# The opening of a two-layer hybrid decoder trunk: a written-out instruction order, three blocks' modulation on TensorE, and six tiles in place of four

## Chip, core and metric

One core of a Trainium2 chip runs the whole kernel in one launch. The metric is device time in microseconds, as the median of several runs. Each kernel also has one profiled execution, whose trace the views are taken from.

## The reference

A trunk of two layers works on 512 tokens of 1024 features. Each layer is a SwiGLU feed-forward step, a token mixer (windowed attention, RWKV-7 and a short convolution side by side) and a second feed-forward step. Ahead of each of the three stands an RMS norm with scale and shift that come from a conditioning vector c, and behind it a gate from c:

```python
c_act = jax.nn.silu(c)
mod = (c_act @ w_ada[l] + b_ada[l]).reshape(B, N_MOD, D_MODEL)
sh1, sc1, gt1, sh2, sc2, gt2, sh3, sc3, gt3 = [mod[:, i, None, :] for i in range(N_MOD)]
hn = rms_norm(h, g_ffn1[l]) * (1.0 + sc1) + sh1
h = h + 0.5 * (1.0 + gt1) * swiglu(hn, w_ffn1_in[l], w_ffn1_out[l])
```

All is float32. The change touches only the start of layer 0: the first norm, its scale and shift, and the first columns of `swiglu`'s first product.

## The kernel before

**Layout.** Features lie on the 128 partitions and tokens along the free axis, so `h` is eight blocks `h[0]` to `h[7]` of 128x512. A normalized block k is kept as two parts, `hnH` (rounded) and `hnL` (the rest), and so is each weight slice (`wH`, `wL`). A product of weights and blocks is then three matmuls: high by high, high by low, low by high (`mm3`, L118 to L120). A **tile** n is 128 output columns of the feed-forward's input weights: 8 blocks x 3 products = 24 matmuls of 512 columns into one PSUM bank. Even tiles are gates, odd ones are ups; a pair makes one silu product.

**The opening** (`begin`, from L1309) has to bring the first tiles to TensorE. In turn it

- replicates c over the partitions (eight matmuls, L1369) and applies silu into `crep`,
- squares the blocks on ScalarE (L243), adds the squares on VectorE (L239), and sums over the partitions with four matmuls (`ps_ss`, L1388); then square root on ScalarE (L1391), reciprocal on VectorE (L1392), and 1/rms is spread over the partitions by four matmuls (`ps_rstd`, L1395),
- forms scale and shift of the blocks: `scales` and three of four `shifts` are dot products of a streamed weight tile `wada` with `crep` on VectorE (L188); each second shift is eight one-column matmuls (`ps_ada`, L1345),
- applies them: `z` = h x 1/rms on VectorE (L1350), scale and shift on ScalarE (L1352), and the split into `hnH` (ScalarE, L130) and `hnL` (VectorE, L132); the weight splits go through the same two lines,
- runs tiles 0 to 3, four blocks' pairs after each other (m = 0 to 3), 96 matmuls.

Matmuls on a tile of ones (`warm`, L1361) fill gaps on TensorE. SP's queue issues the loads: x, then `wada` and the four `wfirst` weight slices in turns.

**Behind it** comes the first feed-forward (`ffn`). Its `projector` takes the four accumulators and goes on with tile 4; each tile's weights are loaded on SP's queue (L292), split on ScalarE and VectorE (L130, L132) into one of four buffer pairs, and multiplied. With each pair of tiles VectorE does a silu product (L513) and its split (L515). At pairs 2 and 3 (j of 2 and 3, of 8) `ada_steps` computes the gate's eight modulation columns: four dot products on VectorE each time, with `wada` tiles that GpSimd's queue loads (L199) into three slots, and with `crep` read back from DRAM (L194), where the opening stored it (L1371). The scheduler behind the tile framework sets the order on each engine from the order of the code and the dependencies; each engine runs its own list in order.

Of the kernel before, what the change touches and what calls it, by code (L numbers as in the profile page):

```python
# [8 lines left out]
F32 = mybir.dt.float32  # L9
# [22 lines left out]
PAD = 24  # L32
GROUPS = ((0, 12), (12, 22))
# [26 lines left out]
def trunk_kernel(ctx, tc, ins, out, layers=L, phases=("ffn1", "mix", "ffn2")):  # L60
# [280 lines left out]
    def ffn(l, w_in, w_pair, w_out, hn, im, ss, need, then, first, ready, coming):  # L341
# [6 lines left out]
        with tc.tile_pool(name="act", bufs=1) as ap_:  # L348
# [153 lines left out]
            for g, (j0, j1) in enumerate(GROUPS):  # L502
                for p in range(j0 // 2, j1 // 2):
                    if p < n_first:
                        X = new_x(p)
                        for j in (2 * p, 2 * p + 1):
# [10 lines left out]
                            if n_first == 4:  # L517
                                ada_steps(ap_, crep, (0, 0, 4, 4, 0, 0, 0, 0)[j], behind)
# [789 lines left out]
    def begin(pool):  # L1308
# [3 lines left out]
        col = {n: pool.tile([P, KD], F32, name=n, tag=n) for n in ("sc", "sh", "gb", "gm0", "sh0")}  # L1312
        stt(col["gb"], bsc, 1.0, g1, ALU.add, ALU.mult)
        wa, wf, ws = {}, [], []

        def fetch(m):
            for n in (0, 2):
                w = pool.tile([P, 2, D], F32, name="wada", tag="wada", bufs=8)
                nc.sync.dma_start(w, ins["wa0"][m, :, n : n + 2])
                wa[m, n], wa[m, n + 1] = w[:, 0], w[:, 1]  # L1320
# [7 lines left out]
        def split_w(n):  # L1328
            pair = tuple(wp.tile([P, KD, P], F32R, name=x, tag=x, bufs=4) for x in ("wH", "wL"))
            split(*pair, wf[n])  # L1330
            ws.append(pair)

        def scales(m):
            for n in range(2):
                k = slice(2 * m + n, 2 * m + n + 1)
                ada_dot(col["sc"][:, k], wa[m, n], crep)
                stt(col["gm0"][:, k], col["sc"][:, k], g1[:, k], col["gb"][:, k], ALU.mult, ALU.add)

        def shifts(m):
            k0, k1 = (slice(2 * m + n, 2 * m + n + 1) for n in range(2))  # L1340
            ada_dot(col["sh"][:, k0], wa[m, 2], crep)
            tt(col["sh0"][:, k0], col["sh"][:, k0], bsh[:, k0], ALU.add)
            pt = psum([P, 1], "ps_ada")
            for k in range(KD):
                mm(pt, wa[m, 3][:, k * P : (k + 1) * P], cact[:, k : k + 1], start=k == 0, stop=k == KD - 1)  # L1345
            tt(col["sh0"][:, k1], pt, bsh[:, k1], ALU.add)

        def normed(k):
            z = E("z")
            tt(z, h[k], rstd, ALU.mult)  # L1350
            x = E("hn_t")
            act(x, z, AF.Identity, bias=col["sh0"][:, k : k + 1], scale=col["gm0"][:, k : k + 1])  # L1352
            split(*hn[k], x)

        pw = psum([P, T], "ps_warm", "r1")
        wide = ones_r.unsqueeze(1).to_broadcast([P, 4, P])

        def warm(n):

            for _ in range(n):  # L1360
                mm(pw.rearrange("p (a b) -> p a b", b=P), ones_r, wide, start=True, stop=True)  # L1361

        warm(3)

        crep = pool.tile([P, D], F32, name="crep", tag="crep")
        for hf in range(2):
            pt = psum([P, 4, P], "ps_crep")
            for k in range(4):
                mm(pt[:, k], cT[:, 4 * hf + k : 4 * hf + k + 1].to_broadcast([P, P]), cst("ident"), start=True, stop=True)  # L1369
            act(crep[:, hf * 512 : hf * 512 + 512], pt.rearrange("p k n -> p (k n)"), AF.Silu)  # L1370
# [9 lines left out]
        nc.sync.dma_start(con[:, P:], ins["con"][:, P:])  # L1380
        warm(20)
        ss = new_ss()
        for i in range(KD):
            add_ss(ss, i)

        pt = psum([P, NB], "ps_ss")
        for b in range(NB):
            mm(pt[:, b : b + 1], ss[:, b * P : (b + 1) * P], ones[:, :1], start=True, stop=True)  # L1388
        warm(3)
        r = pool.tile([P, NB], F32, name="rstd_t", tag="rstd_t")  # L1390
        act(r, pt, AF.Sqrt, bias=vals["eps"], scale=1.0 / D)  # L1391
        nc.vector.reciprocal(r, r)  # L1392
        rstd = psum([P, T], "ps_rstd", "r0")
        for b in range(NB):
            mm(rstd[:, b * P : (b + 1) * P], r[:, b : b + 1].to_broadcast([P, P]), cst("ident"), start=True, stop=True)  # L1395
        warm(2)
        scales(0)
        shifts(0)
        warm(8)
        normed(0)  # L1400
        split_w(0)
        split_w(1)
        normed(1)
        pts = [psum([P, T], "ps_mm", tag) for tag in ("mm", "mm", "r1", "r0")]
        for m in range(4):
            groups = [(n, 2 * m + k) for k in range(2) for n in range(4)]
            if m == 0:
                groups = [(n, k) for n0 in (0, 2) for k in range(2) for n in (n0, n0 + 1)]
            elif m == 3:
                groups = [(n, 6 + k) for n in range(4) for k in range(2)]  # L1410
            for g, (n, k) in enumerate(groups):
                mm3(pts[n], ws[n], k, hn[k], ALL, k == 0, k == KD - 1)
                if m < 3 and g == 1:
                    scales(m + 1)
                    shifts(m + 1)
# [120 lines left out]
```

## Time and profile before

| | |
|---|---|
| median of 3 runs | 1811.94 us (1808.89 to 1813.52) |
| profiled execution | 1810.68 us, span 1808.9 us |
| mean granted TensorE clock | 0.996 |
| TensorE, VectorE, ScalarE, GpSimd busy | 98%, 75%, 46%, 8% of the span |
| chain that ended last | TensorE 85%, VectorE 8%, ScalarE 3%, DMA 2% |

The granted clock is the share of full speed that TensorE was allowed in a stretch. The chain that ended last follows the last instruction back, at each step to what released it. In rows of the timeline stand start, duration, engine, line, operation, output and inputs, shapes and count, and in brackets how long the engine had been idle and what ended that.

### The profile page before, as it was taken

How to read it: one execution, taken by the hardware profiler on the slowest of the kernel's cores; microseconds unless marked ns; L12 is line 12 of the kernel's file. 1: busy time of each engine (PE TensorE's matmuls, PEld its weight loads, DVE VectorE, ACT ScalarE, POOL GpSimd, SP SyncE). 2: the span in 40 equal slices, each digit the busy share in tenths (PEclk: the TensorE clock that was granted, in tenths of full speed). 3: DMA queues.
4: the chain of work that ended last, by engine and by line, in shares of the span. 5: the costliest groups of instructions: out<-in, count | busy, mean ns of one | idle time of the engine just before them, and what ended most of it. 6: DMA issues, size and time to landing. Idle time of an engine off the chain costs nothing.

```text
span 1808.9 us, 33704 instructions
## 1 busy us (share of the span) xinstructions
PE 1779.8 (98%) x13856; PEld 1624.5 (90%) x13856; DVE 1353.8 (75%) x2188; ACT 839.8 (46%) x1292; POOL 141.9 (8%) x225
## 2 busy tenths in 40 slices
PE   8999999999999999999999999999999999999999
PEld 6899899987768999899899989999877799999998
DVE  7687677877768877777877786877696698864862
ACT  4443255374443554255355524544654445533541
POOL 0001110101000001100100010110000000010000
PEclk9999999999999999999999999999999999999999
DMA  8667876713123576967737687773321427684742
GB/s 330 227 166 222 258 193 199 239 65 94 62 84 119 152 192 197 297 180 200 247 110 202 171 293 199 192 229 120 123 65 40 137 83 200 183 247 129 197 140 71
DMA packets 91980, 309.93 MB, mean 171 GB/s; under 512 B 10480, under 2 KB 11248, under 8 KB 90800
## 3 DMA queue, kind: packets, MB, share of 16 engines
q1 hardware_dynamic: 62496, 201.58, 32.6%
q0 software_dynamic: 29328, 106.18, 23.4%
q8 instruction: 109, 1.79, 0.4%
q14 instruction: 47, 0.39, 0.1%
HBM read 303.79 MB, written 3.93 MB: 170 GB/s over the span
## 4 chain that ended last, share of the span: by engine, by line
PE 85%; DVE 8%; ACT 3%; DMA 2%; issue 1%; POOL 0%; ACTq 0%; DVEq 0%; SPq 0%; POOLq 0%
PE ps_mm L118 14%; PE ps_mm L119 14%; PE ps_mm L120 14%; PE ps_d L422 7%; PE ps_d L424 7%; PE ps_d L423 7%; PE ps_f L424 3%; PE ps_f L423 3%; PE ps_f L422 3%; PE ps_g L424 2%; PE ps_g L423 2%; PE ps_g L422 2%; DVE wL L132 2%; DVE wada L188 1%; ACT wH L130 1%
## 5 line engine op out<-in xcount | busy, mean ns | idle before, releaser
L130 ACT CAST wH<-wraw 128x1024 fp32r<-128x1024 f32 (+2 forms) x292 | 266.0, 917 | 466.7 <-PE ps_mm L119 219.0
L132 DVE TENSOR_TENSOR wL<-wraw,wH 128x1024 fp32r<-128x1024 f32 (+2 forms) x292 | 308.3, 1060 | 118.9 <-ACT wH L130 117.5
L118 PE MATMUL ps_mm<-actH,wH 128*128 128x512 f32 (+1 forms) x784 | 281.0, 358 | 0.0
L120 PE MATMUL ps_mm<-actH,wL 128*128 128x512 f32 (+1 forms) x784 | 280.6, 358 | 0.0
L119 PE MATMUL ps_mm<-actL,wH 128*128 128x512 f32 (+1 forms) x784 | 280.5, 358 | 0.0
L118 PE MATMUL ps_mm<-hnH,wH 128*128 128x512 f32 (+1 forms) x760 | 266.1, 357 | 7.1 <-ACT hnH L130 2.9
L119 PE MATMUL ps_mm<-hnL,wH 128*128 128x512 f32 (+1 forms) x760 | 265.9, 352 | 0.3
L120 PE MATMUL ps_mm<-hnH,wL 128*128 128x512 f32 (+1 forms) x760 | 264.0, 350 | 0.6 <-DVE wL L132 0.6
L422 PE MATMUL ps_d<-comH,wH 128*128 128x256 f32 x816 | 225.2, 276 | 0.0
L423 PE MATMUL ps_d<-comL,wH 128*128 128x256 f32 x816 | 224.4, 275 | 0.0
L424 PE MATMUL ps_d<-comH,wL 128*128 128x256 f32 x816 | 224.4, 275 | 0.0
L188 DVE SCALAR_TENSOR_TENSOR wada<-wada,crep 128x1024 f32<-128x1024 f32 x140 | 167.6, 1219 | 30.0 <-DMA wada<-in_wadaT 29.9
L132 DVE TENSOR_TENSOR wL<-sum,wH 128x1024 fp32r<-128x1024 f32 x102 | 125.0, 1225 | 85.4 <-ACT wH L130 85.4
L118 PEld LDWEIGHTS ps_mm<-hnH,wH 128*128 128x128 f32 x760 | 142.9, 191 | 30.0 <-issue 7.6
L120 PEld LDWEIGHTS ps_mm<-actH,wL 128*128 128x128 f32 x784 | 148.7, 190 | 16.9 <-DVE wL L132 0.3
L118 PEld LDWEIGHTS ps_mm<-actH,wH 128*128 128x128 f32 x784 | 148.7, 190 | 16.6
L119 PEld LDWEIGHTS ps_mm<-actL,wH 128*128 128x128 f32 x784 | 148.7, 190 | 16.6
L120 PEld LDWEIGHTS ps_mm<-hnH,wL 128*128 128x128 f32 x760 | 145.4, 191 | 15.6 <-DVE wL L132 1.1
L119 PEld LDWEIGHTS ps_mm<-hnL,wH 128*128 128x128 f32 x760 | 145.3, 191 | 15.5 <-DVE hnL L281 1.0
L422 PEld LDWEIGHTS ps_d<-comH,wH 128*128 128x128 f32 x816 | 156.6, 192 | 1.6 <-ACT s L448 1.6
L424 PEld LDWEIGHTS ps_d<-comH,wL 128*128 128x128 f32 x816 | 156.7, 192 | 0.0
L423 PEld LDWEIGHTS ps_d<-comL,wH 128*128 128x128 f32 x816 | 156.6, 192 | 0.0
(366 smaller groups left out, 3742.9 us busy)
## 6 DMA issues: line engine op xcount, KB each, us to landing
wada<-in_wadaT POOLq DMA_DIRECT2D x128, 512.0 KB, 4.7
wraw<-in_wmi SPq DMA_DIRECT2D x40, 512.0 KB, 3.5
wraw<-in_w2p SPq DMA_DIRECT2D x36, 512.0 KB, 4.4
wraw<-in_w1p SPq DMA_DIRECT2D x32, 512.0 KB, 4.5
wraw<-in_w1o SPq DMA_DIRECT2D x32, 384.0 KB, 4.6
wraw<-in_w2o SPq DMA_DIRECT2D x32, 384.0 KB, 4.3
wraw<-in_w1i SPq DMA_DIRECT2D x20, 512.0 KB, 4.7
wraw<-in_w1o SPq DMA_DIRECT2D x32, 320.0 KB, 3.8
```

Source lines behind the costliest of these rows:

```text
L118: mm(acc, wH, xH, start=start, stop=False)
L119: mm(acc, wH, xL, start=False, stop=False)
L120: latest["large"] = mm(acc, wL, xH, start=False, stop=stop)
L130: nc.scalar.copy(hi, src)
L132: return nc.vector.tensor_sub(lo, src, hi.bitcast(F32))
L188: stt(w, w, 1.0, crep, ALU.mult, ALU.mult, accum_out=out_)
L422: mm(acc, wH, xH, start=start and i + k == 0, stop=False, skip_group_check=True)
L423: mm(acc, wH, xL, start=False, stop=False, skip_group_check=True)
L424: mm(acc, wL, xH, start=False, stop=k == 3, skip_group_check=True)
```

## The change

`begin` is rewritten. Its loops are replaced by a table `PLAN`, a list of 213 short tokens; a function `step` emits one instruction (or a small group) per token, and `pin` ties each instruction on TensorE, VectorE and ScalarE to the one before it on its engine, so that each engine's list is the order of the table. The tokens: `z`, `x`, `H`, `L` with a block number are the multiplication by 1/rms, scale and shift, and the two halves of the split; `wH`, `wL` with a tile number the weight split; `P13c` is tile 1, block 3, third product; `W4` four warm-up matmuls; `d`, `e` the dot products for scale and shift of a block.

- Blocks 0, 1 and 2 get scale and shift from TensorE: `ada` streams a block's 256 modulation columns through eight float32 matmuls of 32 output rows each, which go in turns to four groups of 32 partitions of one bank; `part` copies the bank to SBUF, `col` sums it over the partitions, `gm` adds gain and bias. The stationary operand is `cz`, silu(c) in every 32nd column and zeros between. Blocks 3 to 7 have two dot products each on VectorE.
- The sum of squares stays on TensorE: every block's squares go through four one-column matmuls of their own (32 instead of 4). ScalarE and VectorE share the squares.
- Six tiles (0 to 5) instead of four are computed in the opening, so `projector` goes on with tile 6. The accumulators take all six banks of three PSUM tags.
- x is loaded in four pairs of blocks, `wada` and the six `wfirst` slices one after the other; six of these loads wait for a buffer of an earlier one.
- `crep` is stored to DRAM behind the opening's last VectorE instruction instead of at its start.
- The eight gate columns in `ffn` move from j of 2 and 3 to j of 0 and 1.

```diff
+PLAN = """
+z0 ada0 z1 z7 part0 wH0 W1 col0 z6 gm0 z2 W4 ada1 z4 x0 z3 H0 wL0 part1 P00a wH1 col1 L0 P00c P10a gm1 P00b P10b wL1 x1 ada2 H1 z5 P10c part2 P01a L1
...
-    for i in range(KD):
-        t = hp_.tile([P, T], F32, name=f"h{i}")
-        nc.sync.dma_start(t, ins["xT"][i])
-        h.append(t)
+    for i in range(0, KD, 2):
+        t = hp_.tile([P, 2, T], F32, name=f"h{i}")
+        nc.sync.dma_start(t, ins["xT"][i // 2])
+        h += [t[:, 0], t[:, 1]]
...
-                                ada_steps(ap_, crep, (0, 0, 4, 4, 0, 0, 0, 0)[j], behind)
+                                ada_steps(ap_, crep, (4, 4, 0, 0, 0, 0, 0, 0)[j], behind)
...
+        def pin(e, m):
+            if e in behind:
+                tc.add_manual_dep(m.ins, behind[e].ins.name, ORDER, reason="the opening keeps its order")
+            behind[e] = m
+            return m
...
+        cz = pool.tile([P, KD, CH // 2], F32, name="cz", tag="cz")
+        nc.gpsimd.memset(cz, 0.0)
+        nc.gpsimd.tensor_copy(cz[:, :, 0], cact)
...
-        nc.gpsimd.dma_start(silu_c, crep)
-        fetch(0)
-        fetch_w()
-        fetch_w()
-        fetch(1)
-        fetch_w()
-        fetch_w()
-        fetch(2)
-        fetch(3)
-        warm(20)
-        ss = new_ss()
-        for i in range(KD):
-            add_ss(ss, i)
-        for b in range(NB):
-            mm(pt[:, b : b + 1], ss[:, b * P : (b + 1) * P], ones[:, :1], start=True, stop=True)
...
+        for _ in range(4):
+            fetch()
+            fetch_w()
+        def summed(i):
+            for b in range(NB):
+                m = mm(pt[:, b : b + 1], sqs[i][:, b * P : (b + 1) * P], ones[:, :1], start=i + b == 0, stop=i == KD - 1, skip_group_check=True)
+                pin("PE", m)
+        summed(0)
+        summed(1)
+        for i in range(2, KD):
+            sqs.append(E("sq"))
+            if i in (5, 7):
+                pin("ACT", act(sqs[i], h[i], AF.Square))
+            else:
+                pin("DVE", tt(sqs[i], h[i], h[i], ALU.mult))
+            if i % 2 == 0:
+                warm(4)
+            summed(i)
+        warm(3)
...
-        pts = [psum([P, T], "ps_mm", tag) for tag in ("mm", "mm", "r1", "r0")]
-        for m in range(4):
...
+        more = {"ada0": (fetch,), "ada1": (fetch, fetch_w), "ada2": (fetch,), "wL1": (fetch_w,), "e3": (fetch,)}
...
+            elif kind == "ada":
+                sums[k] = psum([P, 2 * P], "ps_ada")
+                for i in range(KD):
+                    j = slice(i % 4 * 32, i % 4 * 32 + 32)
+                    pin("PE", mm(sums[k][j], cz[:, i], wa[k][:, i * 2 * P : (i + 1) * 2 * P], start=i < 4, stop=i >= 4))
+            elif kind == "part":
+                part[k] = pool.tile([P, 2 * P], F32, name="part", tag="part", bufs=2)
+                pin("ACT", nc.scalar.copy(part[k], sums[k]))
+            elif kind == "col":
+                sums[k] = psum([P, 2], "ps_col")
+                for i in range(2):
+                    pin("PE", mm(sums[k][:, i : i + 1], part[k][:, i * P : (i + 1) * P], ones[:, :1], start=True, stop=True))
+            elif kind == "gm":
+                finish(c, sums[k][:, :1], sums[k][:, 1:])
...
+        for token in PLAN:
+            step(token)
+        kept = nc.gpsimd.dma_start(silu_c, crep)
+        tc.add_manual_dep(kept.ins, behind["DVE"].ins.name, SYNC, reason="after the opening's loads")
+        return hn, [pts[n] for n in range(6)]
```

What this makes of the lists of instructions is seen best at two places. TensorE from the replication of c (`ps_crep`) to the first main matmuls (`ps_mm`), before:

```order
L1369 MATMUL ps_crep<-con,cT 128x128 x8
L1361 MATMUL ps_warm<-ones_r 128x512 x25
L1388 MATMUL ps_ss<-ones_r,ss 128x1 x4
L1361 MATMUL ps_warm<-ones_r 128x512 x8
L1395 MATMUL ps_rstd<-con,rstd_t 128x128 x4
L1345 MATMUL ps_ada<-cact,wada 128x1 x8
L118 MATMUL ps_mm<-hnH,wH 128x512 x2
L119 MATMUL ps_mm<-hnL,wH 128x512
```

The same stretch of TensorE with the change (row counts are matmuls; a float32 matmul shows as two in the trace):

```order
L1360 MATMUL ps_crep<-con,cT 128x128 x8
L1374 MATMUL ps_ss<-ones_r,sq 128x1 x8
L1350 MATMUL ps_warm<-ones_r 128x512 x4
L1374 MATMUL ps_ss<-ones_r,sq 128x1 x8
L1350 MATMUL ps_warm<-ones_r 128x512 x4
L1374 MATMUL ps_ss<-ones_r,sq 128x1 x8
L1350 MATMUL ps_warm<-ones_r 128x512 x4
L1374 MATMUL ps_ss<-ones_r,sq 128x1 x8
L1350 MATMUL ps_warm<-ones_r 128x512 x3
L1394 MATMUL ps_rstd<-con,rstd_t 128x128 x4
L1442 MATMUL ps_ada<-wada,cz 32x256 x8
L1350 MATMUL ps_warm<-ones_r 128x512
```

The sums of squares moved in between the warm-ups, eight groups of four, and the modulation of block 0 is one stream of 256 columns behind the spread of 1/rms.

VectorE behind the opening's last `hnL`, before: `wL` are the weight splits of tiles 4 and up, `wada` the gate's dot products.

```order
L132 TENSOR_TENSOR wL<-wraw,wH 128x1024
L513 SCALAR_TENSOR_TENSOR silu<-silu,ps_mm 128x512 x2
L132 TENSOR_TENSOR wL<-wraw,wH 128x1024
L515 TENSOR_TENSOR actL<-silu,actH 128x512 x2
L132 TENSOR_TENSOR wL<-wraw,wH 128x1024 x3
L513 SCALAR_TENSOR_TENSOR silu<-silu,ps_mm 128x512
L132 TENSOR_TENSOR wL<-wraw,wH 128x1024
L515 TENSOR_TENSOR actL<-silu,actH 128x512
L188 SCALAR_TENSOR_TENSOR wada,mod_2_594<-wada,crep 128x1024 x3
L132 TENSOR_TENSOR wL<-wraw,wH 128x1024
```

With the change VectorE's list at the same place starts with tile 6's split:

```order
L141 TENSOR_TENSOR wL<-wraw,wH 128x1024
L522 SCALAR_TENSOR_TENSOR silu<-silu,ps_mm 128x512 x3
L524 TENSOR_TENSOR actL<-silu,actH 128x512
L141 TENSOR_TENSOR wL<-wraw,wH 128x1024
L524 TENSOR_TENSOR actL<-silu,actH 128x512
L197 SCALAR_TENSOR_TENSOR wada,mod_2_585<-wada,crep 128x1024
L524 TENSOR_TENSOR actL<-silu,actH 128x512
L197 SCALAR_TENSOR_TENSOR wada,mod_2_585<-wada,crep 128x1024 x2
L141 TENSOR_TENSOR wL<-wraw,wH 128x1024
L197 SCALAR_TENSOR_TENSOR wada,mod_2_585<-wada,crep 128x1024
L141 TENSOR_TENSOR wL<-wraw,wH 128x1024
```

Before, the splits of tiles 4 to 9 stood ahead of the first gate dot; now those of tiles 6 and 7 do, and three dots stand ahead of tile 8's split, a fourth ahead of tile 9's.

More of the change, by code (lines that the diff above doesn't have):

```diff
@@ L1326, in fetch_w @@
             wf.append(w)
[L1328 to L1355, printed above, removed]
+        pw = psum([P, T], "ps_warm", "mm")
         wide = ones_r.unsqueeze(1).to_broadcast([P, 4, P])
```

120 lines of the change are left out of this document (77 added, 43 removed).

## The prediction

> **What bounds the kernel now.** I read the page's head first, for the size of the thing.
>
> ```profile
> span 1808.9 us, 33704 instructions
> PE 1779.8 (98%) x13856; PEld 1624.5 (90%) x13856; DVE 1353.8 (75%) x2188; ACT 839.8 (46%) x1292; POOL 141.9 (8%) x225
> ```
>
> TensorE (PE) is busy 98% of the span. The profiled execution took 1810.68 us, its span and 1.8 us around it; the three timed runs have their median at 1811.94, 1.3 above. All that the change rewrites lies in the first 4% of the span, so I cut the opening into slices, and then asked whom PE waits for in the first 160 us (beside 2.4 us for the first instruction of all).
>
> ```profile
> 0.00:15.00 15.00, 12.62 (x55) 10.99 (x56) 5.38 (x15) 10.08 (x16) 0.90 (x5) 1.00 0.85 303
> 15.00:20.00 5.00, 3.94 (x30) 3.60 (x29) 4.99 (x12) 0.52 (x1) 0.00 (x0) 1.00 1.01 419
> 20.00:25.00 5.00, 3.03 (x6) 2.05 (x7) 3.74 (x5) 4.04 (x6) 0.00 (x0) 0.69 1.01 422
> 25.00:30.00 5.00, 3.83 (x25) 3.23 (x23) 5.00 (x13) 1.70 (x2) 0.00 (x0) 0.97 1.03 422
> 30.00:35.00 5.00, 3.85 (x11) 3.17 (x12) 4.92 (x6) 2.96 (x5) 0.00 (x0) 0.71 1.01 418
> 35.00:40.00 5.00, 5.00 (x31) 4.50 (x31) 2.85 (x9) 0.00 (x0) 0.00 (x0) 0.95 0.96 383
> ```
>
> ```profile
> PE ps_mm L118 <- ACT hnH L130: 2.9, 1, 2.9
> PE ps_mm L118 <- ACT wH L130: 2.5, 2, 2.3
> ```
>
> The columns are PE, weight load, VectorE (DVE), ScalarE (ACT), GpSimd, then the granted PE clock, the DMA share and GB/s. From 15 to 35 us PE is idle 5.4 us, 5.4 us of it in waits for normalized blocks and split weights, and in two slices its clock stands at 0.69 and 0.71, which loses another 5 x 0.31 + 5 x 0.29 = 3.0 us. DVE is full there. The end of this stretch is the place to compare: when are the first six tiles (0 to 5, 24 matmuls each) done?
>
> ```profile
> 54.98 0.38 PE L118 MATMUL ps_mm<-hnH,wH 128*128 128x512 f32 x1
> ...
> 61.89 0.38 PE L120 MATMUL ps_mm<-hnH,wL 128*128 128x512 f32 x1
> ```
>
> The first row is tile 4's first matmul, the second stands 32 matmuls later: 6.91 / 32 = 0.216 us each. Before, tiles 4 and 5 end 48 matmuls after 54.98, at **65.35 us**. From there the order of the matmuls is the same in both kernels, and those waits were all up to 160 us. So the gain is 65.35 minus the new end of six tiles, called T6, less what later tiles give back.
>
> **The change, step by step.** First the way to 1/rms.
>
> ```profile
> 3.83 3.62 PE L1369 MATMUL ps_crep<-con,cT 128*128 128x128 f32 x16
> 7.10 6.45 PE L1361 MATMUL ps_warm<-ones_r 128*128 128x512 f32 x25
> 13.38 1.03 PE L1388 MATMUL ps_ss<-ones_r,ss 128*128 128x1 f32 x8
> 14.28 2.09 PE L1361 MATMUL ps_warm<-ones_r 128*128 128x512 f32 x8
> 16.20 1.05 PE L1395 MATMUL ps_rstd<-con,rstd_t 128*128 128x128 f32 x8
> ```
>
> ```profile
> 14.45 0.26 ACT L1391 ACTIVATE rstd_t<-ps_ss,v_eps 128x4 f32<-128x4 f32 x1 [1.95 <-PE ps_ss L1388]
> 14.75 0.18 DVE L1392 RECIPROCAL rstd_t<-rstd_t 128x4 f32<-128x4 f32 x1 [1.44 <-ACT rstd_t L1391]
> ```
>
> ```profile
> 17.37 0.68 DVE L1350 TENSOR_TENSOR z<-h,ps_rstd 128x512 f32<-128x512 f32 x1
> 17.97 1.22 DVE L188 SCALAR_TENSOR_TENSOR wada<-wada,crep 128x1024 f32<-128x1024 f32 x1
> ```
>
> The additions at L239 leave DVE, and PE sums each block's squares instead: eight groups like the one at 13.38, one after the other (the next row begins 0.90 after it, so 0.90 each), with twelve warm-up matmuls between them. They cannot start before the replication of c ends, at 7.45. 7.45 + 8 x 0.90 + 12 x 0.216 = 17.25; square root and reciprocal take 0.44, with their handovers 0.6, and the replication of 1/rms 1.05: z begins near **19.1 instead of 17.37**. This step loses 1.7 us. The table load for the square root goes earlier, beside the wait for blocks, and costs nothing. The paired loads of x move the same bytes, and GpSimd, 8% busy, has filled cz long before 18 us: nothing either; a late cz would delay the first stream one for one.
>
> Then block 0's modulation. DVE did it before, with dot products like the one at 17.97 (a z takes 0.60 from its start to the next instruction's, a dot 1.14 by the same measure). What follows it on ACT and DVE stays, in the durations of these rows:
>
> ```profile
> 19.48 0.81 ACT L1352 ACTIVATE hn_t<-z,sh,gm 128x512 f32<-128x512 f32 x1 [4.77 <-DVE sh L1342]
> 20.20 1.03 ACT L130 CAST wH<-wfirst 128x1024 fp32r<-128x1024 f32 x1
> 21.14 0.61 ACT L130 CAST hnH<-hn_t 128x512 fp32r<-128x512 f32 x1
> 21.26 1.23 DVE L132 TENSOR_TENSOR wL<-wfirst,wH 128x1024 fp32r<-128x1024 f32 x1 [1.28 <-ACT wH L130]
> ```
>
> For the new part, the nearest rows are a later product in two column groups, and a copy of 256 columns out of PSUM:
>
> ```profile
> 1419.38 1.08 PE L650 MATMUL ps_av<-pmc,V 128*64 128x512 f32 x4
> 1420.29 1.03 PE L650 MATMUL ps_av<-pmp,V 128*64 128x512 f32 x4
> ```
>
> ```profile
> L1173 ACT COPY Sc<-ps_sc x24: 372/376/379, 452.3 to 1399.2; 128x256 f32<-128x256 f32 x24
> ```
>
> The new streams (eight float32 matmuls of 32 output rows by 256 columns, two passes each) stand nowhere in this trace. A float32 pass takes twice a column's normal time (0.216 per 512), so 256 columns take 0.216 a pass. Bounds: one after the other, 16 x 0.216 = 3.5 us; four column groups fully side by side, 0.9. The nearest row is ps_av: four passes of 512 columns in two groups of 64, 0.91 us from first to next, where in sequence they would take 1.7. So groups do run beside each other, and I take **1.0** with the switch. By the Trainium skill's "TensorEngine Tiling (Array Packing)", Key Properties, changing the tiling mode drains TensorE, which speaks against three short streams among full-width matmuls; if each of six switches cost the 0.16 by which a matmul's 0.38 exceeds its pitch, that is 1.0, and 0.7 more than the 0.1 a stream that I count; no row here shows such an order.
>
> Onward: PE streams block 0 from 18.9 to 19.9; ACT copies the sums (0.38, to 20.35); two column sums on PE to 20.85. DVE does four z meanwhile (4 x 0.60, to 21.5), then scale and shift (0.3): 21.8. ACT: 0.81 and 0.61, so the first main matmul starts at **23.3**. DVE follows with three z, wL, hnL, block 1's scale and shift, wL, z and hnL: 3 x 0.60 + 1.14 + 0.60 + 0.30 + 1.14 + 0.60 + 0.60 = 6.2, to 28.0, and in that time PE does two more streams, the column sums and eight main matmuls, with gaps. From then on I find every operand ready before its turn: 136 matmuls and three warm-ups, 139 x 0.216 = 30.0, give **T6 = 58.1**. The thinnest margin is tile 3's low weights, 0.2 us ahead; for what slips I add 0.4: **58.5**.
>
> DMA hides: eight streams of 1.05 MB, six tiles of 0.52 MB and 2.3 MB of inputs are 13.8 MB. Adding up the slices above, 13.0 MB had moved by 35 us and 14.9 by 40, so the last stream lands near 38; its dot product's turn is near 43. On SP's queue these loads wait for ada0, wL0, ada1, wL1, ada2 and block 3's second dot, done by 33 us. Cover gone, each microsecond of lateness is a microsecond of T6.
>
> So the opening gains 65.35 - 58.5 = 6.85 us. Now what comes after. Tile 6's weights wait for tile 0's buffer, as tile 4's did; no change. But the eight gate columns' dots move two tile pairs up, and their loads, POOL's and the reload of c on SP, now wait for T6, because they fall on memory that the opening's last matmul reads.
>
> ```profile
> 48.56 0.33 SPq L194 DMA_DIRECT2D crep<-silu_c  x1
> ```
>
> ```profile
> 48.85 1.58 POOL L199 DMA_DIRECT2D wada<-in_wadaT  x3 [39.76 <-ACT hn_t L1352]
> 71.87 0.53 POOL L199 DMA_DIRECT2D wada<-in_wadaT  x1 [21.44 <-DVE wada L188]
> 73.02 0.53 POOL L199 DMA_DIRECT2D wada<-in_wadaT  x1 [0.62 <-DVE wada L188]
> 74.17 0.53 POOL L199 DMA_DIRECT2D wada<-in_wadaT  x1 [0.62 <-DVE wada L188]
> ```
>
> ```profile
> 76.33 1.23 DVE L188 SCALAR_TENSOR_TENSOR wada<-wada,crep 128x1024 f32<-128x1024 f32 x1 [1.32 <-DMA wada<-in_wadaT]
> ...
> 81.75 1.23 DVE L188 SCALAR_TENSOR_TENSOR wada<-wada,crep 128x1024 f32<-128x1024 f32 x1 [0.51 <-DMA wada<-in_wadaT]
> ```
>
> ```profile
> wada<-in_wadaT POOLq DMA_DIRECT2D x128, 512.0 KB, 4.7
> ```
>
> Before, the first of these loads went out at 48.9, and the reload of c at 48.6, some 20 us ahead of need. Now DVE meets the dots with the loads just issued; queued behind them on DVE are the weight splits of tiles 8 to 11, for which PE waits. From a load's issue to its dot, L, it took 4.5 us for the fourth (71.87 to 76.33) and 7.6 for the sixth (74.17 to 81.75), where DVE stood waiting for them; the median of all 128 loads is 4.7. Three slots serve eight dots, so tile 10's split comes three rounds after T6: 3L + 6.0 (three dots of 1.14, two reissues estimated at 0.4, one subtraction of 0.60, the split of 1.14, and 0.1 to start), and PE wants it at T6 + 4 x 5.18 + 0.43 = T6 + 21.2. With L = 5.06 that is even; each 1 us more costs 3. I take L = 5.4, between the median and the mean of the three (5.6): **1.0 us** given back (0 to 7.6). Tile 8's split is then 0.1 from its limit, and the Strassen-like pairs after tile 15 have DVE some 5 us less ahead than before, which I count within that range.
>
> Sum: 1810.68 - 6.85 + 1.0 = 1804.8, forecast **1805** (1806.1 set against the median instead).
>
> **The rivals.**
>
> Given back: L = 7.5 as in the slowest row holds tile 10 for 7 us; time about 1811. For it: one of two rows, and in the new order the reload of c and two weight loads share the DMA engines. Against: the median of 128. 15%.
>
> The streams don't overlap: 3 x 2.5 = 7.5 us more, T6 = 66, time 1812, so the change doesn't do what it says. Against it stands ps_av. 7%.
>
> The clock: between 8 and 17 us PE now runs 1.8 us of one-column sums to every 0.86 of warm-ups. Before, the slices that fell to 0.69 and 0.71 followed about 2 us of small matmuls and idling, and each cost 1.5 us. Three such falls in the new opening cost 4.5: 1809.3. By the Trainium skill's "TensorE: Matmul & The Clock Gate", Part 1, a free-running window of about 3.4 us decides and an idle one halves the clock; whether one-column matmuls count as idle it doesn't say, and no row here isolates them. 8%.
>
> Slower: the same place, one mechanism: if the gate loads take L = 9.2 us or more, tile 10 waits 12.4, which eats the 6.85 and 5.5 on top: 1816 and up. It decides from L = 9.2; the longest seen is 7.6. 8%.
>
> **How the numbers follow.** Forecast 62%, its own range 1801 to 1806: T6 may be 2 us earlier if nothing slips and nothing is given back, or a little later. The three middle cases, 30%, end from 1809 to 1812, and the last has 8%. A 0.3% step, 5.4 us, is about what a measurement of this kernel can tell from no change: faster 0.62, within it 0.30, slower 0.08. The range of 8 in 10 takes in the middle cases and, below, a T6 of 56 with a run at the low end of the three (3 us under the median): 1798.5 to 1813.
>
> **What would show it.** z starts at 19 (wrong if at 17 or 21); a stream takes about 1.0 on PE; first main matmul at 23 to 24; six tiles done at 58 to 59; granted clock 1.0 from 20 to 35; PE's only later waits for wL at tiles 8 and 10, a microsecond in all. A stream of 3 us, cold slices before 30, or waits of several microseconds between 69 and 85 would prove the forecast wrong, each with its rival; so would late streams on DVE near 40 (a DMA bound).

## The result: slower by 0.44%, and the profile after

The changed kernel took 1819.59 us (median of 11 runs, 1815.97 to 1822.75) against 1811.68 (11 runs, 1808.89 to 1815.70): a ratio of **1.0044, 95% interval 1.0033 to 1.0055**. Its profiled run took 1815.97 us, the fastest of the eleven. The same slices of the opening, with the columns as before:

```profile
0.00:15.00 15.00, 12.62 (x63) 11.79 (x63) 2.88 (x9) 8.03 (x12) 0.71 (x6) 0.87 0.85 324
15.00:20.00 5.00, 5.00 (x21) 4.61 (x21) 0.00 (x0) 0.00 (x0) 0.00 (x0) 0.50 1.00 408
20.00:25.00 5.00, 5.00 (x21) 4.71 (x22) 0.23 (x2) 0.26 (x1) 0.00 (x0) 0.50 0.83 338
25.00:30.00 5.00, 5.00 (x31) 2.83 (x29) 3.33 (x8) 1.85 (x3) 0.00 (x0) 0.69 0.14 34
30.00:35.00 5.00, 4.75 (x44) 2.52 (x44) 5.00 (x10) 3.88 (x7) 0.00 (x0) 1.00 0.92 370
35.00:40.00 5.00, 5.00 (x27) 4.35 (x26) 4.55 (x8) 3.50 (x5) 0.00 (x0) 1.00 0.99 388
```

TensorE is busy all through, and yet the stretch is lost: its clock stands at 0.50 from about 11 us to 28 (17.1 us by the record), and VectorE and ScalarE have next to nothing to do from 14 us until 23. The timeline of TensorE and the milestones (z, the first stream, the first main matmul, tile 6's first matmul, and VectorE's reciprocal in the norm behind the feed-forward, which stood at 360.26 before):

```profile
7.24 2.05 PE L1374 MATMUL ps_ss<-ones_r,sq 128*128 128x1 f32 x16
9.14 1.17 PE L1350 MATMUL ps_warm<-ones_r 128*128 128x512 f32 x4
...
14.43 3.41 PE L1374 MATMUL ps_ss<-ones_r,sq 128*128 128x1 f32 x16
17.70 2.05 PE L1350 MATMUL ps_warm<-ones_r 128*128 128x512 f32 x4
19.55 3.41 PE L1374 MATMUL ps_ss<-ones_r,sq 128*128 128x1 f32 x16
...
26.08 1.94 PE L1442 MATMUL ps_ada<-wada,cz 128*32 128x256 f32 x16
...
30.08 1.07 PE L1442 MATMUL ps_ada<-wada,cz 128*32 128x256 f32 x16
31.08 0.48 PE L1419 MATMUL ps_mm<-hnH,wH 128*128 128x512 f32 x1
```

```profile
26.19 2.48 DVE L1425 TENSOR_TENSOR z<-h,ps_rstd 128x512 f32<-128x512 f32 x4 [2.67 <-PE ps_rstd L1394]
```

```profile
65.89 0.46 PE L127 MATMUL ps_mm<-hnH,wH 128*128 128x512 f32 x1
```

```profile
365.56 0.17 DVE L274 RECIPROCAL rstd<-rstd 128x2 f32<-128x2 f32 x1 [1.78 <-ACT rstd L273]
```

Two blocks' eight sums (sixteen rows) take 1.9 us at 7.24 and 3.3 at 14.43, counted from a row's start to the next. Six tiles are done at 65.89, 0.5 later than before instead of 6.85 earlier, and by the first norm the kernel is 5.3 behind, which is the whole difference of the two profiled runs (1815.97 - 1810.68 = 5.29). So 4.8 us go between 66 and 366. They show as waits of TensorE, slice by slice and row by row:

```profile
60.00:100.00 40.00, 36.94 (x170) 31.55 (x169) 25.81 (x38) 14.82 (x19) 4.25 (x8) 1.00 0.62 217
100.00:140.00 40.00, 38.99 (x254) 35.95 (x253) 35.59 (x43) 21.54 (x26) 3.96 (x5) 1.00 0.70 186
```

```profile
78.72 0.48 PE L129 MATMUL ps_mm<-hnH,wL 128*128 128x512 f32 x1 [1.79 <-DVE wL L141]
90.61 0.48 PE L129 MATMUL ps_mm<-hnH,wL 128*128 128x512 f32 x1 [1.27 <-DVE wL L141]
```

The same slices before were full:

```profile
60.00:100.00 40.00, 40.00 (x187) 35.04 (x186) 32.66 (x48) 14.19 (x18) 4.37 (x7) 1.00 0.76 228
100.00:140.00 40.00, 39.99 (x284) 37.66 (x283) 30.92 (x34) 21.99 (x28) 2.23 (x3) 1.00 0.53 153
```

The waits are 3.1 + 1.0 = 4.1 us; the other 0.7 is spread too thin to be located. The 3.1 stand at tiles 8 and 10 (78.72 and 90.61), behind splits that VectorE reaches late; the 1.0 stands in the pair stage, near 128 us. That VectorE is late, and not the weights, shows at tile 8: ScalarE has the high half of its weights ready at 70.2, but VectorE works off three dots first, and the third of them has to wait for its load before tile 8's split comes.

```profile
69.20 1.04 ACT L139 CAST wH<-wraw 128x1024 fp32r<-128x1024 f32 x1
```

```profile
76.30 1.23 DVE L197 SCALAR_TENSOR_TENSOR wada<-wada,crep 128x1024 f32<-128x1024 f32 x1 [0.65 <-DMA wada<-in_wadaT]
...
77.45 1.22 DVE L141 TENSOR_TENSOR wL<-wraw,wH 128x1024 fp32r<-128x1024 f32 x1
```

Where the gate's work begins:

```profile
66.12 0.33 SPq L203 DMA_DIRECT2D crep<-silu_c  x1
```

```profile
66.76 1.59 POOL L208 DMA_DIRECT2D wada<-in_wadaT  x3 [8.89 <-ACT silu L520]
```

```profile
63.94 1.23 DVE L141 TENSOR_TENSOR wL<-wraw,wH 128x1024 fp32r<-128x1024 f32 x1 [7.10 <-ACT wH L139]
...
72.66 1.23 DVE L197 SCALAR_TENSOR_TENSOR wada<-wada,crep 128x1024 f32<-128x1024 f32 x1 [2.55 <-DMA wada<-in_wadaT]
```

The gate's loads go out at T6, as foreseen (48.6 and 48.9 before). VectorE stands idle for 7.1 us ahead of tile 6's split, whose buffer tile 0 holds until 62.9, three microseconds before the opening's end, and again for 2.6 us until the first gate weights land.

### The profile page after: what moved, and what is told of

Its sections match the earlier page's. It is cut to its first block, busy times and chain, and to the rows that moved or that the text cites. A ratio compares the mean times of both kernels' runs of the same rounds, so it can differ in the third digit from the quotient of the medians.

```text
span 1814.2 us, 33785 instructions
## 1 busy us (share of the span) xinstructions
PE 1785.9 (98%) x13898; PEld 1629.1 (90%) x13898; DVE 1347.8 (74%) x2181; ACT 840.0 (46%) x1292; POOL 142.8 (8%) x227
## 4 chain that ended last, share of the span: by engine, by line
PE 80%; DVE 9%; DMA 4%; ACT 4%; issue 2%; POOL 0%; ACTq 0%; DVEq 0%; SPq 0%; POOLq 0%
PE ps_mm L127 12%; PE ps_mm L128 12%; PE ps_mm L129 12%; PE ps_d L431 7%; PE ps_d L432 7%; PE ps_d L433 7%; PE ps_f L432 3%; PE ps_f L433 3%; PE ps_f L431 3%; DVE wL L141 2%; PE ps_g L432 2%; PE ps_g L433 2%; PE ps_g L431 2%; PE ps_mm L1419 2%; DMA wada<-in_wadaT 2%
## 5 line engine op out<-in xcount | busy, mean ns | idle before, releaser
L129 PE MATMUL ps_mm<-hnH,wL 128*128 128x512 f32 (+1 forms) x712 | 245.0, 346 | 3.6 <-DVE wL L141 3.6
L127 PE MATMUL ps_mm<-hnH,wH 128*128 128x512 f32 (+1 forms) x712 | 247.3, 354 | 1.3 <-ACT hnH L289 0.9
L128 PE MATMUL ps_mm<-hnL,wH 128*128 128x512 f32 (+1 forms) x712 | 246.2, 348 | 0.1
L197 DVE SCALAR_TENSOR_TENSOR wada<-wada,crep 128x1024 f32<-128x1024 f32 x128 | 153.5, 1221 | 37.5 <-DMA wada<-in_wadaT 37.3
L139 ACT CAST wH<-sum 128x1024 fp32r<-128x1024 f32 x102 | 106.8, 1047 | 105.0 <-PE ps_f L432 42.4
L127 PEld LDWEIGHTS ps_mm<-hnH,wH 128*128 128x128 f32 x712 | 133.5, 191 | 21.5 <-issue 7.6
L129 PEld LDWEIGHTS ps_mm<-hnH,wL 128*128 128x128 f32 x712 | 135.6, 190 | 17.8 <-DVE wL L141 4.8
```

Source lines behind the costliest of these rows:

```text
L127: mm(acc, wH, xH, start=start, stop=False)
L128: mm(acc, wH, xL, start=False, stop=False)
L129: latest["large"] = mm(acc, wL, xH, start=False, stop=stop)
L139: nc.scalar.copy(hi, src)
L197: stt(w, w, 1.0, crep, ALU.mult, ALU.mult, accum_out=out_)
```

## The experiments

My theory after reading the two traces was that **two things** cost the time: the halved clock (7 us of z), and the gate's dot products ahead of the splits (4 to 5 us). Rivals: the chain of sums is long for another reason and the clock its consequence; the waits behind T6 come from the weights' own buffers and loads. In the table "lost" is the lateness of the first norm less that of T6, both against the kernel before (65.35 and 360.26); medians stand beside those of the kernel before on the same chip. Kernels with "wide" have the first edit below as well. In six kernels the clock also fell to half at the end of a wait or right behind it, for 3.4 us, which costs 1.7 (wide sums at 72.6 us; dots at j of 2, 3 at 126.0; added sums, dots at 2, 3 at 121.7; wide, dots at 3, 4 at 122.9; narrow, dots late at 158.5), or for 6.8 (six dots early, at 69.5); their "lost" holds that too.

| kernel | z | T6 | norm | lost | median (before) | ratio, interval |
|---|---|---|---|---|---|---|
| changed kernel | 26.19 | 65.89 | 365.56 | 4.8 | 1819.59 (1811.68) | 1.0044, 1.0033 to 1.0055 |
| wide sums | 19.30 | 58.44 | 359.87 | 6.5 | 1812.33 (1810.39) | 1.0006, 0.9997 to 1.0015 |
| sums added on VectorE | 20.87 | 60.30 | 359.69 | 4.5 | 1809.41 (1810.39) | 0.9998, 0.9989 to 1.0007 |
| before, narrow warm-ups | 21.65 | - | 365.73 | - | 1816.51 (1810.93) | 1.0032, 1.0021 to 1.0043 |
| more warm-ups | 31.97 | 71.56 | 371.75 | 5.3 | 1826.48 (1810.58) | 1.0093, 1.0079 to 1.0108 |
| dots at j of 2, 3 | 23.43 | 62.56 | 365.14 | 7.7 | 1818.60 (1810.39) | 1.0045, 1.0028 to 1.0061 |
| added sums, dots at 2, 3 | 19.41 | 58.55 | 359.12 | 5.7 | 1811.68 (1810.39) | 1.0007, 0.9997 to 1.0017 |
| wide, freed loads | 18.88 | 58.01 | 357.05 | 4.1 | 1810.65 (1810.93) | 0.9991, 0.9980 to 1.0002 |
| wide, dots at 3, 4 | 18.91 | 58.04 | 361.62 | 8.7 | 1813.78 (1810.93) | 1.0016, 1.0003 to 1.0028 |
| wide, freed, dots at 3, 4 | 18.91 | 58.05 | 359.29 | 6.3 | 1813.14 (1810.93) | 1.0002, 0.9991 to 1.0012 |
| wide, dots late | 18.69 | 57.82 | 354.69 | 2.0 | 1808.48 (1811.94) | 0.9990, 0.9980 to 1.0000 |
| narrow, dots late | 29.09 | 68.22 | 369.46 | 6.3 | 1821.62 (1810.01) | 1.0060, 1.0046 to 1.0073 |
| wide, freed, 4 dots early | 19.24 | 58.37 | 355.88 | 2.6 | 1809.11 (1811.94) | **0.9982, 0.9974 to 0.9991** |
| wide, freed, 6 dots early | 19.45 | 58.59 | 362.50 | 9.0 | 1814.23 (1811.94) | 1.0013, 1.0004 to 1.0023 |
| wide, freed, 2 early, 6 late | 18.94 | 58.08 | 355.94 | 3.0 | 1809.27 (1810.58) | 0.9998, 0.9986 to 1.0010 |

### The clock

**Wide sums**: the same 32 matmuls, with 128 columns of ones.

```diff
-m = mm(pt[:, b : b + 1], sqs[i][:, b * P : (b + 1) * P], ones[:, :1], ...)
+m = mm(pt[:, b], sqs[i][:, b * P : (b + 1) * P], ones, ...)
```

> The changed kernel with one edit: each of the 32 matmuls that sum the squares streams 128 columns of ones instead of one column; weights loaded, order and number of instructions stay. Theory: one-column matmuls leave TensorE so little occupied that its clock is halved from 11 to 28 us. With 128 columns the clock stays at 1.00 from 8 us on, z begins at 19 to 20 instead of 26.2, six tiles are done at 59 to 60 instead of 65.9, and the median falls by 6 to 7, to about 1813. Rival: the chain of sums is long for another reason (squares or blocks of x that arrive late, weight loads of float32), and the low clock is its consequence; then z stays at 25 or later, the clock low, and the time at 1819 to 1821.

TensorE's timeline, the slices, and the milestones of this kernel (z, the first main matmul, tile 6):

```profile
12.89 1.95 PE L1374 MATMUL ps_ss<-ones_r,sq 128*128 128x128 f32 x16
```

```profile
15.00:20.00 5.00, 5.00 (x47) 4.02 (x45) 0.93 (x4) 0.26 (x1) 0.00 (x0) 1.00 1.01 410
20.00:25.00 5.00, 4.34 (x39) 2.48 (x31) 5.00 (x10) 4.05 (x6) 0.00 (x0) 1.00 1.03 423
```

```profile
19.30 2.48 DVE L1425 TENSOR_TENSOR z<-h,ps_rstd 128x512 f32<-128x512 f32 x4 [1.20 <-PE ps_rstd L1394]
```

```profile
23.53 0.48 PE L1419 MATMUL ps_mm<-hnH,wH 128*128 128x512 f32 x1
```

```profile
58.44 0.46 PE L127 MATMUL ps_mm<-hnH,wH 128*128 128x512 f32 x1
```

128 times the columns, and the sums run faster, since the clock holds. The opening comes out as predicted (19.1, 23.3, 58.5), and the median stands 1.9 above the kernel before instead of 7.9. The clock is the cause, not the consequence; that much is shown. What is lost behind the opening grew from 4.8 to 6.5 all the same: TensorE waited 3.2 us at tile 8 (72.65), and the clock was then halved for 3.4 us.

**Sums added on VectorE**, as before the change, with ScalarE's squares and twenty warm-ups meanwhile.

```diff
-            if i % 2 == 0:
-                warm(4)
-            summed(i)
...
+        warm(20)
...
+            pin("DVE", tt(ss, ss, sq, ALU.add))
```

> The changed kernel with the sums of squares as before the change: ScalarE squares, VectorE adds, twenty warm-up matmuls on TensorE meanwhile, four matmuls at the end. Theory of the halved clock: z begins at 17.5 to 18.5, the clock is 1.00 from 8 to 28 us, six tiles are done near 57.5, the median falls by about 7 to 8, to 1812. Rival (the loads set the opening): z begins early, but the streams or weight splits then wait for their loads and six tiles are still done after 63; the median stays at 1817 or more.

The median, 1809.4, is lower than the 1812 of the text, but the profiled opening missed it: TensorE, done with its warm-ups, waited 3.3 us for the last addition, the clock fell for 6.8 us, z began at 20.87 (17.5 to 18.5 expected), and T6 was 60.3. The rival, loads that keep T6 behind 63, is out.

**Narrow warm-ups in the kernel before**: twenty of its 33 stream one column; the other thirteen are pinned where they stood.

```diff
-        warm(20)
+        for _ in range(20):
+            last = mm(pw[:, :1], ones, ones[:, :1], start=True, stop=True)
...
```

> The kernel before, with the first 20 of its 33 warm-up matmuls streaming one column of float32 instead of 512, about as long (0.22 us each by the sums' rows) and in the same place. Theory: one-column matmuls do not hold the clock, however busy TensorE looks. Then the clock falls to 0.50 within 8 to 20 us, the chain of square root, reciprocal and spread runs longer, z begins 1 to 3 us later than 17.4, and the time rises by 1 to 4. Rival: any stream of matmuls and weight loads holds the clock; then the clock stays at 1.00 until 20 us and the time is that of the kernel before.

```profile
10.00:15.00 5.00, 5.00 (x23) 4.61 (x23) 3.10 (x6) 2.61 (x4) 0.00 (x0) 0.57 1.03 410
15.00:20.00 5.00, 5.00 (x17) 4.23 (x17) 2.70 (x7) 0.26 (x1) 0.00 (x0) 0.50 1.02 421
```

The clock fell (1.00 in these slices before), z came 4.3 us later, and the time rose by 5.6, both more than the text gave (1 to 3 and 1 to 4). The effect does not need the rest of the change.

**More warm-ups** between narrow sums.

```diff
-            if i % 2 == 0:
-                warm(4)
+            warm(4)
             summed(i)
```

> The changed kernel with four warm-up matmuls ahead of every block's narrow sums from block 2 on, where before it was ahead of every second block: 24 instead of 12, so that wide matmuls fill about half of the time between 9 and 22 us instead of a quarter. Theory that the share of wide matmuls sets the clock: it stays at 1.00 or falls for at most one stretch of 3.4 us; the 12 added matmuls cost 2.6 us at full clock, z begins at 21 to 24, six tiles are done near 61, and the time is 1814 to 1816, faster than the changed kernel although it does more. Rival (any one-column sum keeps the clock down, or the wide sums helped in another way): the clock is halved as in the changed kernel, the added matmuls cost 5 us, z begins at 29 to 33 and the time is 1822 to 1825.

```profile
18.36 2.05 PE L1350 MATMUL ps_warm<-ones_r 128*128 128x512 f32 x4
20.21 1.70 PE L1374 MATMUL ps_ss<-ones_r,sq 128*128 128x1 f32 x8
21.77 2.05 PE L1350 MATMUL ps_warm<-ones_r 128*128 128x512 f32 x4
```

The rival was right, though the time, 1826.5, lies above the 1822 to 1825 that it gave: the clock was halved for 23.9 us, and z came another 5.8 us later. Warm-ups fill 1.85 of every 3.41 us here (18.36 to 20.21, and again from 21.77), and that is not enough to bring the clock back.

### What is lost behind the opening

**Dots at j of 2 and 3 again**, alone and with the added sums.

```diff
-ada_steps(ap_, crep, (4, 4, 0, 0, 0, 0, 0, 0)[j], behind)
+ada_steps(ap_, crep, (0, 0, 4, 4, 0, 0, 0, 0)[j], behind)
```

> The changed kernel with one edit: the eight gate columns stand at j of 2 and 3 again. Theory: of the loss, one part is the halved clock in the opening and another is what TensorE waits behind the gate dots (1.8 us at tile 8, 1.3 us at tile 10, another 1 us in the pair stage at 120 to 140 us, 4.1 us in all in the changed kernel's profile). Then these waits go, the opening stays as it is (six tiles done at 65.9), and the median falls by about 4, from 1819.6 to some 1815.5. Rival: the waits are only slack of a late opening and something later takes their place; then less than 1.5 us is gained and the median stays at 1818 or more.

> Both edits together: the squares added on VectorE as before, and the gate columns at j of 2 and 3 as before. What stays of the change are the fixed order, the three streams and the six tiles. If the two causes are separate, the gains add: about 7.5 and 4, so near 1808, faster than the kernel before by 3 to 4. Rival: they are not separate (one late thing hides the other); then it is no better than the better of the two alone, about 1812.

Both missed; the numbers that came are those of the rivals (1818 or more, about 1812). With six tiles in the opening, the pair of j = 2 is done at T6 as well, so three of the first four dots still stand ahead of tile 8's split, and TensorE waited 1.9 us there in the first kernel (75.50). The edit did not undo what I thought it undid.

**Freed loads**: the weights of tiles 4 and 5 and the pair stage's buffers get pools of their own.

```diff
-                home, bufs = (wp, 4) if k < 4 else (pool, 2)
+                home, bufs = (wp, 4) if k < 4 else (late, 2)
-        with tc.tile_pool(name="act", bufs=1) as ap_:
+        with tc.tile_pool(name="com", bufs=8) as cp_, tc.tile_pool(name="act", bufs=1) as ap_:
```

> The kernel with wide sums, and in it the weights of tiles 4 and 5 in memory of their own that only the combination buffers of the pair stage take over, so that the gate's loads and the reload of c no longer wait for the opening's last matmul. They should go out near 51 to 53 us instead of 58.7 and 59.3. Theory: what later stages give back (with wide sums the six tiles are done 6.9 us earlier than in the kernel before, but the first norm behind the feed-forward only 0.4 earlier: 6.5 us lost between 58 and 360) comes from loads that wait for the sixth tile. Then the first norm comes at 354 to 356 instead of 359.9, TensorE's wait of 3.2 us at 70 to 73 is gone, and the median falls from 1812.3 to about 1808. Rival: the loss comes from where the dots stand on VectorE (now even three of them ahead of tile 7's split and five ahead of tile 8's); then the wait stays or grows and the time is 1812 or more.

The reload of c and the first loads went out at 52.53 and 53.10, and the eight gate loads then took 5.2 us to land in the median, against 7.0 with wide sums alone. The loss fell from 6.5 to 4.1, about half of what the theory asked for (median 1810.7 instead of 1808); 1.7 of that is the stretch at half clock, which did not come here. Dots whose weights were there still stood ahead of the splits:

```profile
66.28 0.48 PE L129 MATMUL ps_mm<-hnH,wL 128*128 128x512 f32 x1 [1.43 <-DVE wL L141]
72.10 0.48 PE L129 MATMUL ps_mm<-hnH,wL 128*128 128x512 f32 x1 [0.80 <-DVE wL L141]
```

**Dots at j of 3 and 4**, without and with freed loads.

```diff
-ada_steps(ap_, crep, (4, 4, 0, 0, 0, 0, 0, 0)[j], behind)
+ada_steps(ap_, crep, (0, 0, 0, 4, 4, 0, 0, 0)[j], behind)
```

> The kernel with wide sums, and the eight gate columns at j of 3 and 4 instead of 0 and 1, which puts them behind the split of tile 9, as far behind the opening's end as before the change; their loads still wait for the sixth tile, but have 15 us more until they are needed. Theory of place (dots that wait for their loads stand ahead of the splits of tiles 8 to 11): the waits at 70 to 100 us are gone, the first norm comes at 354 to 356, the median falls to about 1808. Rival one (the weights' own loads are late, having two raw buffers and the same DMA engines): waits of 2 to 3 us stay there, 1811 to 1813. Rival two (the dots then collide with the sums for the pair stage): the waits move to 110 to 140 us, same time.

> Both edits of the two kernels above: loads freed from the sixth tile, and the dots behind tile 9's split. If either cause alone explains the loss, this is as fast as the better one, about 1807 to 1808, and no faster; if each carries a part, it is faster than both, down to 1805 (the first norm at 353, as the whole opening gain of 6.9 would make it); if neither does, 1812.

The second rival of the first text was right, and with freed loads the time, 1813.1, is the one that the second text gave for neither cause (1812). The first kernel's slices:

```profile
60.00:100.00 40.00, 40.00 (x187) 34.81 (x185) 28.81 (x44) 12.95 (x17) 4.92 (x8) 1.00 0.74 252
100.00:140.00 40.00, 35.14 (x245) 32.81 (x245) 32.94 (x38) 21.68 (x27) 2.26 (x3) 0.96 0.63 168
```

No wait to 100 us, then 4.9 us of them: the dots now collide with the sums that VectorE forms for the pair stage.

**Dots late**: none beside tiles and pairs, with wide and with narrow sums.

```diff
-ada_steps(ap_, crep, (4, 4, 0, 0, 0, 0, 0, 0)[j], behind)
+ada_steps(ap_, crep, (0, 0, 0, 0, 0, 0, 0, 0)[j], behind)
```

> The kernel with wide sums, and no gate dot at all beside the tiles and the pair stage: the eight columns are computed when that half of the feed-forward's columns is done, from some 190 us on. Theory (VectorE is the bound between 58 and 130 us: what it must do there for TensorE, dots included, takes as long as before, and TensorE now comes 6.9 us earlier): without the 9.2 us of dots TensorE waits less than 1 us between 58 and 150, and reaches 150 us about 6 us ahead of the kernel before. What comes after depends on the dots at 190: if TensorE waits there for the gate, the time is 1811 or more all the same; if not, the first norm comes at 354 to 355 and the median is 1806 to 1808. Rival (raw weight buffers and DMA set the pace): 2 us of waits or more remain between 60 and 140.

> The changed kernel, narrow sums and all, with no gate dot beside the tiles and the pair stage (the fourth corner beside the changed kernel, the one with wide sums, and the one with wide sums and late dots). Theory of two separate causes: the opening stays as slow as in the changed kernel (z at 23 to 26, six tiles done at 62.5 to 66), TensorE's waits between 66 and 140 us, 4.1 us, are gone, a wait of 1.8 us near 150 comes; the first norm comes at 358 to 362 instead of 365.6 and the median falls by 3 to 4 from 1819.6, to about 1816. Rival: with an opening this late VectorE has room again, and the dots cost nothing; then less than 1.5 is gained.

With wide sums, the slices and the one wait left:

```profile
60.00:100.00 40.00, 40.00 (x188) 35.01 (x187) 30.93 (x39) 18.59 (x23) 1.72 (x2) 1.00 0.62 184
100.00:140.00 40.00, 39.99 (x315) 38.60 (x314) 29.23 (x35) 20.85 (x27) 4.36 (x7) 1.00 0.64 181
```

```profile
146.77 0.38 PE L431 MATMUL ps_d<-comH,wH 128*128 128x256 f32 x1 [1.80 <-DVE up L470]
```

The first norm comes 5.6 us ahead of the kernel before. The 1.8 us of wait are more than the text allowed (1), and the median is just above its range. With the dots their loads left this stretch too; that the dots' place on VectorE counts is seen in the rows at 69.20 and 77.45 of the changed kernel. So the waits from 58 to 140 are the gate's and not the weight buffers'; that is shown for the kernel with wide sums. With narrow sums the waits at tiles 8 and 10 went too, but nothing was gained: the opening of the profiled run was 2.3 us later still, TensorE waited 2.3 at 157 and the clock fell there for 3.4 us, and it waited 2.1 at the norm. There my text, which gave 1816, missed: the time was 1821.6.

**Dots in VectorE's idle stretch**: with freed loads, c stored at the start, and 4, 6 or 2 dots ahead of everything; of the others, two or four at j of 3, or all six late.

```diff
+            if crep:
+                ada_steps(ap_, crep, 4)
...
-ada_steps(ap_, crep, (4, 4, 0, 0, 0, 0, 0, 0)[j], behind)
+ada_steps(ap_, crep, (0, 0, 0, 4, 0, 0, 0, 0)[j], behind)
```

> The kernel with wide sums and with loads freed from the sixth tile, c stored at the start again, and the dots divided: four are issued ahead of everything, so that two fall into VectorE's idle stretch of some 8 us ahead of tile 6's split, and four at j of 3. Theory of VectorE as the bound: 4.6 us of dots leave the crowded stretch, so of the 6.5 us lost there 3 to 5 come back; first norm at 355 to 356.5 instead of 359.9, median 1807 to 1808.5. Rival: the dots ahead of tile 6's split make that split late and TensorE waits at 58 to 60; then 1811 or more.

> As the kernel with four early dots, but six early and two at j of 3. Theory of VectorE as the bound: the two more stand between the silu products and make the splits of tiles 7 and 8 late by up to 2.3 us, where the slack is smallest, while the pair stage gets 2.3 us back; near the kernel with four, 1807 to 1810. Rival (only the pair stage matters): faster than with four by 1 to 2.

> As the kernel with wide sums and no dots beside the tiles, but with loads freed from the sixth tile and two of the eight dots ahead of tile 6's split, in VectorE's idle stretch before 58 us; six dots stay for the time from 150 us on. Theory of VectorE as the bound: no wait above 0.5 us between 60 and 140 us; the wait of 1.8 us near 147 shrinks, since two dots fewer stand there; first norm at 352.5 to 354.5 (360.3 in the kernel before), median 1806 to 1808. Rival: the two early dots delay tile 6's split, TensorE waits 0.8 us at 58 and as much as before at 147; then 1808.5 or more.

With four, TensorE waited 0.8 us at tile 6 and 1.4 at tile 7, and no more until 340; the median is 0.6 above the text's range. This is the one version that **beats the kernel before** clear of the noise: by 0.18% (0.09 to 0.26), where the changed kernel was 0.44% slower. It is the best of fourteen edits, and not told apart from wide sums with late dots (0.9990, 0.9980 to 1.0000). With six, TensorE had waited 1.7 and 4.3 us by 71, and the clock fell for 6.8; the text, 1807 to 1810, missed (1814.2). With two, the rival was right: TensorE waited 1.0 us at tile 6 and 1.6 at 148. There the profiled run is quicker still (span 1804.0, against 1805.0 with four), but its runs spread from 1805.7 to 1815.0, and their median is not told apart from the kernel before.

## Why the prediction was wrong, step by step

- **What bounds the kernel**: right; the opening could be made 6.9 us shorter.
- **The way to 1/rms: this step failed.** It priced 8 x 0.90 + 12 x 0.216 us at the full clock and got 19.1 for z; with the clock held, z came at 19.30. In the changed kernel it came at 26.19, since the sums themselves halved the clock. I had this as a rival, three falls of 1.5 us at 8%. The mechanism was right, the size and the chance were not: one stretch of 17.1 us, which cost z 7.1. The row it was priced from, four sums behind twenty-five wide warm-ups, had been measured with the clock already up.
- **Streams, first main matmul, six tiles**: right in size. At the full clock a stream took 1.00 us from its start to the next row (1.0 predicted; 30.08 to 31.08), with wide sums the first main matmul stood at 23.53 (23.3) and T6 at 58.44 (58.5). The groups do run side by side.
- **DMA hides**: right; VectorE never waited for a stream of block 3 or later, and TensorE's only wait from 30 to 66 us was 0.2 for a split.
- **What later tiles give back: this term was mis-sized.** The place was right, tiles 8 and 10, but TensorE waited 3.1 us there for the 1.0 of the sum. It hung on L = 5.4, the time from a load's issue to its dot. On the way to tile 10's split stand the first, the fourth and the seventh load; they took 5.9, 4.4 and 7.5 us, 17.8 for the 3 x 5.4 = 16.2 of the sum, and the first went out 0.9 behind T6 instead of 0.1. 17.8 + 6.0 + 0.8 - 21.2 gives 3.4. Tile 8's split, taken to be just in time, came 1.8 late, since the third load took 8.5. L was taken from a kernel whose gate loads were spread over 33 us (48.9 to 81.5); here they go out within 16 (66.8 to 82.6), beside the reload of c and the tiles' weights. The pair stage, counted within the range, took another 1.0, and 0.7 is not located: 4.8 in all. From issue to landing alone, the eight loads took:

```profile
DMA to landing us min/median/max: 3.9/6.5/8.5
```

- **The cases**: the prediction gave the clock 8% and the late loads 15% as cases that exclude each other; here both came, a case it had no time or chance for. The measured time is close to that of its "slower" case (1816 and up), but that is luck: that case had the opening's gain in full and tile 10 waiting 12.4 us.
- **The sum**: 1810.68 + 0.5 + 4.8 = 1816.0, the profiled run's time. The median is 3.6 above it. Three kernels here have the changed opening word for word (the changed kernel, dots at 2 and 3, narrow with late dots): z came at 26.19, 23.43 and 29.09, after 17.1, 10.2 and some 21 us at half clock. So the same opening differs from one run to another by 5.7 us, enough to cover the 3.6, and the profile caught the fastest of eleven. Where the clock fell in the other ten was not recorded, but their mean granted clock was: the two fastest runs (1815.97 and 1816.50) have 0.993, and seven others, from 1819.5 to 1822.8, have 0.990 to 0.992. Two runs with 0.998 (1818.6 and 1820.6) do not fit; a record that begins late, as below, would explain them.

The runs of one kernel spread over 5 to 10 us (wide sums with late dots from 1804.7 to 1813.6). Single stretches of 3.4 us at half clock come and go behind the opening in every profile, and the record ties them to the spread: from the first norm to the end, the sixteen profiled runs took 1448.0 to 1448.2 us with one such stretch, 1448.6 to 1450.0 with two, and 1452.1 to 1454.9 with three to five (the one that the end of the kernel cuts off not counted). Of the 119 runs of the kernel before that were timed beside the experiments, the 20 with a mean clock of 0.997 or more took 1808.2 in the median, the 28 with 0.994 or less 1812.9. What stays open is what sets these stretches off.

## What to carry over

Price an added instruction with what it does to the clock as well: a stretch of TensorE that looks 100% busy can be at half speed, and widening its matmuls can make it faster. When an engine is sped up ahead of a queue that another engine works off, count that other engine's work to the next meeting point: with four of VectorE's dots ahead of tile 6's split, TensorE waited 2.2 us up to the first norm, with all eight among the tiles 4.4 (two kernels with wide sums), and most other places only moved the wait.

## What the runs showed of the hardware

- Matmuls of one column do not hold TensorE's clock: 32 of them between 12 warm-ups left it at 0.50, the same 32 with 128 columns at 1.00. Once it had fallen, 1.85 us of full-width warm-ups in every 3.41 did not bring it back.
- Every stretch at half clock that a record shows whole lasted a multiple of 3.41 us: 3.4, 6.8, 10.2, 17.1, 23.9. The Trainium skill, "TensorE: Matmul & The Clock Gate", Part 1, says that the deciding window is 3413 ns, runs free, and does not start with the kernel. The trace agrees with the length, and a free phase would explain why one opening was cold for 10 to 21 us. By the same part of the Trainium skill one busy window brings the full clock; it doesn't say how busy, and 54% of a window (1.85 of 3.41 us, above) was not enough here.
- The granted clock of a slice can be wrong at a program's start. In the kernel with narrow sums and late dots the record of the clock begins near 29 us (at 5 to 8 us in the other fifteen profiles), and the slices ahead of it show 1.00; but the matmuls there run at half pace.

```profile
15.00:20.00 5.00, 5.00 (x21) 4.61 (x21) 0.00 (x0) 0.63 (x1) 0.00 (x0) 1.00 1.01 413
```

```profile
12.36 3.41 PE L1374 MATMUL ps_ss<-ones_r,sq 128*128 128x1 f32 x16
15.63 2.05 PE L1350 MATMUL ps_warm<-ones_r 128*128 128x512 f32 x4
```

Sixteen rows in 3.41 us and four warm-ups in 2.05 are what half clock gave above. The duration of a known matmul is the better witness.
